# Hybrid decoder block on one core: the last projection as seven half-size products, with its weight prepared earlier

## The chip, the cores and the metric

One of the eight cores of a Trainium2 chip runs the kernel. The time is that of the device for one execution, in microseconds (us); the compared number is the median of several runs. TensorE multiplies matrices into PSUM, VectorE, ScalarE and GpSimd work on tiles, and sixteen DMA engines move data; SP and ScalarE issue the DMAs from queues that are worked off in order.

## The reference: what is computed

A residual block over 2048 positions of width 1024, all float32: one input projection of the normed input to 8192 columns, a recurrent branch, a dilated attention branch, two branch projections, a merge, and the last projection with a gated residual and a norm.

```python
mod = c_act @ w_mod[l] + b_mod[l]
shift, scale, gate = jnp.split(mod, 3, axis=-1)
h = rms_norm(x, g_norm[l]) * (1.0 + scale[:, None, :]) + shift[:, None, :]
proj = h @ w_in[l]
...
y_rnn = (hr * jax.nn.silu(z_rnn.astype(jnp.float32))).astype(dt) @ w_out_rnn[l]
...
y_attn = (o * jax.nn.silu(z_attn.astype(jnp.float32))).astype(dt) @ w_out_attn[l]
merged = jax.nn.sigmoid(g_r + bg_r) * y_rnn + jax.nn.sigmoid(g_a + bg_a) * y_attn
x = x + gate[:, None, :] * (merged @ w_o[l])
return rms_norm(x, g_final)
```

## The kernel before

Every float32 product is made of three fast matmuls: an operand is split into a high part (a copy to the rounded type, on ScalarE, `hi_act`, L157) and a low part (the difference, on GpSimd `lo_pool`, L163, or VectorE `lo_dve`, L166), and `mm3` (its matmuls all have line 149) adds high x high, high x low and low x high in PSUM. "A split" below means this pair of operations. A matmul has 128 rows of contraction and up to 512 columns.

**Input projection, two halves** (`f` = 0 and 1, each 1024 positions). A half has three stages. First the value products (`value_runs`), while VectorE and ScalarE build the half's operands (`build_odd`, L568 to L590); `second_values` (L862) holds the second half's plan: 8 runs of 4 slots, 24 matmuls of 256 columns a slot, and `plan[t, i]` lists what is issued behind each slot. Then the other columns in pairs of 128, by seven products of half-size blocks in place of eight (`strassen`): names B11, T2, T3, T1, B21, T4, B22, accumulators X, Z, W, V, Y in PSUM, 4 x 3 matmuls of 512 columns a product. 22 pairs lie in the recurrent stage, 6 in the rotary stage (pool `qp`). Operands are loaded and split some products ahead (`events`, `LEAD` = 4; in the second half `load_next` keeps seven tiles ahead, from `sD` or, unsplit, from the input weight). `later(d, fn)` and `after_prod` issue a step d products later. `output_weights` (L435) splits the two branch weights and stores them to `wD`, one part (load, split, store) every 6 products from the second half's start. `residual_gate` (L1253) computes the gate row of `mod` in the second half's rotary stage: eight 1024-wide loads `gw`, eight adds `gacc` on VectorE, two sums over partitions on TensorE, then the row is stored to `gateD`.

**Attention, with the branch projections as filler.** The generator `steps` (L1727) makes 8 jobs: `w_out_rnn` for four blocks of 512 positions, then `w_out_attn` for four. A job has 8 tiles (128 output channels x 512 positions), a tile 8 steps of one `mm3` into a `pj` bank (two banks). Steps are fed in between attention's work (`spend`). A tile's code at step k: at k = 1 and 5 a weight half is loaded (`load_w`), at k = 1 the tile before is evicted by VectorE with the gate tiles `fg` (L1789, L1791), at k = 3 the gates are loaded (`load_g`; four `fg` buffers, two a tile), at k = 7 the tile before is stored to `meT` (L1796). Operand rows `y` are loaded and split ahead (`load_y`, `split_y`). Jobs 0 to 5 lie under attention; a weight half is then read ready split from `wD`.

**The last stretch.** Jobs 6 and 7 read raw weight halves (`wr`, L1743) and split them. `output_operands` (L1901) loads `w_o` by rows, multiplies it with the gate row (L1905) and splits it (`oh`, `ol`). `output(n)` (L1909) takes one group of 128 positions after the other: load x and merged rows `mraw`, split them (`mh`, `ml`), 2 x 8 `mm3` into `pq`, add to x (L1927), square and sum (L1930), the inverse root, scale by it and by `g_final` (L1932), store. Job 7's steps are put between the first groups. This stretch lies outside the hand-written order (`manual_schedule`), so the compiler places its instructions.

Of the kernel before, what the change touches and what calls it, by code (L numbers as in the profile page):

```python
# [20 lines left out]
P = 128  # L21
# [68 lines left out]
def decoder_block(ctx, tc, x, c, positions, g_norm, w_mod, b_mod, w_in, b_gate, conv_w, conv_b,  # L90
# [24 lines left out]
    gateD = scratch("gateD", [1, D])  # L115

# [318 lines left out]
    def output_weights():  # L435

        parts = [(i, w, m, half) for i, w in enumerate((w_out_rnn, w_out_attn)) for m in range(KT) for half in range(2)]
        for x, (i, w, m, half) in enumerate(parts):
# [17 lines left out]
            for d, fn in ((1, load), (4, split), (6, store)):  # L456
                after_prod.setdefault(n_prod[0] + 6 * x + d, []).append(fn)
# [404 lines left out]
    def second_values():  # L862
# [22 lines left out]
        plan[7, 0].append(lambda: next(odd, None))  # L885
        value_runs(vx, ((0, 2), (1, 2), (2, 2), (3, 2), (3, 3), (0, 3), (1, 3), (2, 3)), plan, [])
# [366 lines left out]
    def residual_gate(ep):  # L1253
        acc = T(ep, [P, D], F32, "gacc")
        row = T(ep, [1, D], F32, "grow")
        nc.sync.dma_start(row[:], b_mod[0:1, 2 * D : 3 * D])
        w = {}

        def load(k):
            w[k] = T(ep, [P, D], F32, "gw", bufs=2)  # L1260
            nc.sync.dma_start(w[k][:], w_mod[0, k * P : (k + 1) * P, 2 * D : 3 * D])

        def add(k):
            t = w.pop(k)
            if k == 0:
                nc.vector.tensor_scalar(acc[:], t[:], ca[:, k : k + 1], None, ALU.mult)
            else:
                nc.vector.scalar_tensor_tensor(acc[:], t[:], ca[:, k : k + 1], acc[:], ALU.mult, ALU.add)

        def total(q):  # L1270
            w["pt"] = T(pg, [P, CH], F32, "pg")
            mm(w["pt"][:1, :], ones[:, 0:1], acc[:, q * CH : (q + 1) * CH], True, True)

        def bias(q):
            cq = slice(q * CH, (q + 1) * CH)
            nc.vector.tensor_tensor(row[:, cq], w["pt"][:1, :], row[:, cq], ALU.add)
            if q:
                nc.sync.dma_start(gateD, row[:])

        for k in range(KT):  # L1280
            later(1 + 3 * k, lambda k=k: load(k))
            later(6 + 3 * k, lambda k=k: add(k))
        for q in range(2):
            later(30 + 2 * q, lambda q=q: total(q))
            later(31 + 2 * q, lambda q=q: bias(q))
# [53 lines left out]
    for f in range(2):  # L1339
# [34 lines left out]
        if f:  # L1374
            residual_gate(qp)
# [348 lines left out]
    stored, whole = set(), []  # L1724


    def steps(jobs):  # L1727

        tiles = [(j, m) for j in range(len(jobs)) for m in range(KT)]
        Y, G = {}, {}  # L1730

        def load_w(x):

            if x < 2 * len(tiles):
                assert x == n_w[0]
                j, m = tiles[x // 2]
                if not whole:
                    load_wd(jobs[j][0], m, x % 2)
                    return

                n_w[0] += 1
                W[x] = T(pS, [P, 2, KH, P], F32R, f"S{x % 4}")
                t = T(whole[0], [P, KH, P], F32, "wr", bufs=3)  # L1743
                rows = slice(x % 2 * KH * P, (x % 2 + 1) * KH * P)
                nc.sync.dma_start(t[:], (w_out_rnn, w_out_attn)[jobs[j][0]][0, rows, m * P : (m + 1) * P]
                                  .rearrange("(k p) m -> p k m", p=P))
                hi_act(W[x][:, 0], t[:])
                (lo_dve if x % 2 else lo_pool)(W[x][:, 1], t[:], W[x][:, 0])

        def new_y(j, k):  # L1750
            Y[j, k] = [T(fl, [P, CH], F32R, tag, bufs=NY) for tag in ("yh", "yl")]
            return Y[j, k]

        def load_y(j, k):
            if j < len(jobs):
# [6 lines left out]
                if k in (1, 2, 3, 4):  # L1762
# [39 lines left out]
        for t, (j, m) in enumerate(tiles):  # L1802
            ps = T(pj, [P, CH], F32, "pj")
            for k in range(KT):
                if k % KH == 1:

                    load_w(2 * t + k // KH + 3)
# [4 lines left out]
                if k == 7 and t:  # L1812
# [161 lines left out]
```

## Time and profile before

| | us |
|---|---|
| three runs | 2258.34, 2264.17, 2263.09 |
| their median | 2263.09 |
| the profiled execution | 2262.75 |
| its span in the profile | 2260.8 |
| TensorE busy in the span | 2215.7 |
| mean granted TensorE clock | 0.993 |

The profile gives, for one execution, when each instruction ran, what ended an engine's idle time before it, and when each DMA was issued and landed. A row of a group of instructions has the line, the engine, the operation, output <- input (tile names without numbers), the shape and the count; then the busy time, the mean duration in ns of one, and the idle time of the engine before them with what ended it. Matmuls overlap, so the time of one (390 ns or so) is longer than the distance to the next. PEld is TensorE's weight load, which lies beside its matmuls.

### The profile page before, as it was taken

Reading aid. Unit: us, or ns where it says so; the run is one execution under the profiler, and the core shown is the slowest. Engines: PE = TensorE matmul, PEld = TensorE weight load, DVE = VectorE, ACT = ScalarE, POOL = GpSimd, SP = SyncE. Lnnn points to the kernel's source line nnn. Section 1 sums busy time; section 2 is a strip of 40 time slices with the busy share of each in tenths; the row PEclk is TensorE's granted clock in tenths of the full one; section 3 lists DMA queues with packets and bytes.
Section 4 is the critical chain, followed back from the end, with each engine's and each line's share of the span. In section 5 each row is a group of like instructions: output and inputs, shape, how many; then the busy total and the mean of one; then the engine's idle time right before and its main releaser. Section 6 shows DMA issues by size and latency. Waiting matters only on the chain.

```text
span 2260.8 us, 34143 instructions
## 1 busy us (share of the span) xinstructions
PE 2215.7 (98%) x11454; PEld 1862.4 (82%) x11455; DVE 1397.7 (62%) x2384; ACT 1271.4 (56%) x2475; POOL 1098.1 (49%) x816
## 2 busy tenths in 40 slices
PE   8999999999999999999999999999999999989998
PEld 5998888888877988888888887888888898877886
DVE  5578788777567555455545354466677877666443
ACT  3547667678543546657657412567678877533211
POOL 2267677676567454444444232446566666432100
PEclk9999999999999999999999999999999999999999
DMA  8354665565797456777776999989988797898542
GB/s 283 89 170 170 198 216 179 189 223 191 246 285 222 134 174 214 238 232 224 233 237 215 291 314 280 288 272 281 276 270 259 236 280 228 252 333 264 153 132 88
DMA packets 457235, 512.04 MB, mean 226 GB/s; under 512 B 89606, under 2 KB 341218, under 8 KB 456036
## 3 DMA queue, kind: packets, MB, share of 16 engines
q1 hardware_dynamic: 430452, 431.02, 63.0%
q10 hardware_dynamic: 26416, 78.81, 9.1%
q8 instruction: 90, 1.47, 0.3%
q14 instruction: 85, 0.70, 0.1%
q0 software_dynamic: 192, 0.05, 0.0%
HBM read 336.73 MB, written 173.02 MB: 225 GB/s over the span
## 4 chain that ended last, share of the span: by engine, by line
PE 51%; DMA 8%; DVE 4%; issue 2%; POOL 2%; SPq 1%; ACT 1%; POOLq 0%; ACTq 0%; DVEq 0%
PE pj L149 9%; PE X L149 8%; PE pq L149 7%; PE V L149 7%; PE Z L149 4%; PE W L149 4%; PE Y L149 3%; PE o L149 3%; PE sc L149 3%; DMA vraw<-vN 1%; PE pg L149 1%; PE pT L1574 1%; DMA wr<-in_w_out_attn_dram 1%; DMA S<-wD 1%; DMA yl<-oT 1%
## 5 line engine op out<-in xcount | busy, mean ns | idle before, releaser
L163 POOL TENSOR_TENSOR S<-R,S 128x512 fp32r<-128x512 f32 x246 | 365.2, 1490 | 358.8 <-ACT S L157 308.9
L149 PE MATMUL pj<-yh,S 128*128 128x512 f32 x1024 | 343.1, 395 | 6.9 <-ACT yh L157 4.8
L149 PE MATMUL X<-T,S 128*128 128x512 f32 x1344 | 332.2, 396 | 2.8 <-ACT S L157 1.5
L149 PE MATMUL V<-T,S 128*128 128x512 f32 x1344 | 331.3, 395 | 0.0
L149 PEld LDWEIGHTS X<-T,S 128*128 128x128 f32 x1344 | 253.2, 189 | 64.1 <-ACT S L157 2.5
L149 PEld LDWEIGHTS V<-T,S 128*128 128x128 f32 x1344 | 252.2, 188 | 58.6
L149 PEld LDWEIGHTS pj<-yh,S 128*128 128x128 f32 x1024 | 193.3, 189 | 48.1 <-ACT yh L157 6.0
L157 ACT ACTIVATE S<-R 128x512 fp32r<-128x512 f32 x246 | 150.9, 622 | 107.1 <-DMA R<-in_w_in_dram 92.9
L149 PE MATMUL pj<-yl,S 128*128 128x512 f32 x512 | 201.5, 394 | 2.6 <-DVE yl L166 1.6
L163 POOL TENSOR_TENSOR S<-s,S 128x512 fp32r<-128x512 f32 x84 | 128.5, 1530 | 112.3 <-ACT S L157 82.5
L1490 ACT ACTIVATE pp<-pp,st 128x256 f32<-128x256 f32 (+3 forms) x256 | 133.3, 522 | 74.8 <-DVE st L1489 74.4
L149 PE MATMUL Y<-T,S 128*128 128x512 f32 x672 | 165.5, 395 | 0.0
L149 PE MATMUL W<-T,S 128*128 128x512 f32 x672 | 165.5, 395 | 0.0
L149 PE MATMUL Z<-T,S 128*128 128x512 f32 x672 | 165.5, 395 | 0.0
L149 PEld LDWEIGHTS W<-T,S 128*128 128x128 f32 x672 | 126.3, 188 | 30.3 <-DMA R<-in_w_out_attn_dram 0.9
L149 PEld LDWEIGHTS Z<-T,S 128*128 128x128 f32 x672 | 126.5, 188 | 29.9
L149 PEld LDWEIGHTS Y<-T,S 128*128 128x128 f32 x672 | 126.5, 188 | 29.5
L958 DVE SCALAR_TENSOR_TENSOR xc<-xr,par,xc 128x512 f32<-128x512 f32 x96 | 98.6, 1028 | 50.4 <-ACT xc L952 48.1
L166 DVE TENSOR_TENSOR ptl<-pT,pth 128x384 fp32r<-128x384 f32 (+1 forms) x160 | 97.7, 627 | 48.6 <-ACT pth L157 46.3
L1489 DVE CUSTOM_DVE_ANT_0 pp<-sc,msk 128x256 f32<-128x256 f32 (+3 forms) x256 | 104.1, 448 | 35.5 <-PE sc L149 33.3
L1554 ACT ACTIVATE pp<-pp,M 128x256 f32<-128x256 f32 (+3 forms) x256 | 118.1, 524 | 9.2 <-DVE M L1678 9.2
L163 POOL TENSOR_TENSOR kq<-kraw,kq 128x512 fp32r<-128x512 f32 (+1 forms) x64 | 101.3, 1593 | 40.7 <-ACT kq L157 31.2
(332 smaller groups left out, 4725.2 us busy)
## 6 DMA issues: line engine op xcount, KB each, us to landing
sD<-S ACTq DMA_DIRECT2D x118, 512.0 KB, 3.7
S<-sD SPq DMA_DIRECT2D x118, 512.0 KB, 4.8
S<-wD SPq DMA_DIRECT2D x99, 512.0 KB, 5.8
R<-in_w_in_dram SPq DMA_DIRECT2D x196, 256.0 KB, 4.1
wD<-s ACTq DMA_DIRECT2D x64, 256.0 KB, 5.1
T<-in_w_mod_dram SPq DMA_DIRECT2D x8, 1024.0 KB, 12.1
vN<-ev SPq DMA_DIRECT2D x64, 128.0 KB, 2.0
zaT<-ev SPq DMA_DIRECT2D x32, 256.0 KB, 2.8
```

The costliest lines, as they stand in the source:

```text
L149: nc.tensor.matmul(o, lhsT=l, rhs=r, start=st, stop=sp, **kw)
L157: nc.scalar.activation(o, i, AF.Copy)
L163: nc.gpsimd.tensor_tensor(o, i, h.bitcast(F32), ALU.subtract)
L166: nc.vector.tensor_tensor(o, i, h.bitcast(F32), ALU.subtract)
L958: nc.vector.scalar_tensor_tensor(xc, xr[:, i : i + CH], cw(i), xc, ALU.mult, ALU.add)
L1489: nc.vector.tensor_tensor_reduce(pdst, s_ps, mask, 1.0, 3e38, ALU.add, ALU.min, m_)
L1490: nc.scalar.activation(pdst, pdst, AF.Exp, bias=m_, scale=-1.0, accum_out=l_)
L1554: nc.scalar.activation(pp, pp, AF.Copy, scale=w)
L1574: nc.tensor.transpose(pt[:, c0 + j * P : c0 + (j + 1) * P], pp[i][:, k * P : (k + 1) * P], ident)
```

## The change

- **The last projection by seven products.** `output_products` takes two groups of 128 positions and both 512-column halves of the weight at a time, by the scheme of `strassen`: 8 pairs x 7 products x 12 matmuls. The merged rows are loaded, summed (VectorE) and split (ScalarE, GpSimd) some products ahead (`jobs`, `LEAD`); GpSimd adds the shared sums u2 and u3 to x; V alternates between a bank of its own and one of `pj`. The last pair has shorter final operations (`finish_last`).
- **The gate row** is computed during the second half's value products, in 512-column halves: a load `gw` behind one slot, the add three slots later.
- **The gated weight.** `gated_weight`, in the second half's rotary stage, loads `w_o` in four groups of rows, multiplies it with the gate row, forms the sums that the seven products need and stores seven parts to `oD` on ScalarE's queue. They are loaded and split late, during jobs 6 and 7 (`load_o`, `hi_o`, `lo_o`), the last eight of 28 splits behind the first products.
- **Jobs 6 and 7 share each weight**: their tiles alternate (two and two at the start), and a weight half is loaded and split once for both; 12 halves are raw, the others come from `wD`. Their store comes at k = 5.
- **The branch weights'** parts come every 19/4 products, not every 6.
- All of the last stretch now lies in the hand-written order. `output_operands`, `output` and the pools `pq` and `wr` are gone.

```diff
-                after_prod.setdefault(n_prod[0] + 6 * x + d, []).append(fn)
+                after_prod.setdefault(n_prod[0] + 19 * x // 4 + d, []).append(fn)
...
+        residual_gate(vx, plan)
         value_runs(vx, ((0, 2), (1, 2), (2, 2), (3, 2), (3, 3), (0, 3), (1, 3), (2, 3)), plan, [])
...
+    def residual_gate(ep, plan):
...
-        for k in range(KT):
-            later(1 + 3 * k, lambda k=k: load(k))
-            later(6 + 3 * k, lambda k=k: add(k))
+            nc.vector.tensor_tensor(row, w["pt"][:1, :], row, ALU.add)
+            nc.scalar.dma_start(gateD[:, q * CH : (q + 1) * CH], row)
+
         for q in range(2):
-            later(30 + 2 * q, lambda q=q: total(q))
-            later(31 + 2 * q, lambda q=q: bias(q))
+            for k in range(KT):
+                i = 2 + 13 * q + (3 * k) // 2
+                at_slot(i, lambda q=q, k=k: load(q, k))
+                at_slot(i + 3, lambda q=q, k=k: add(q, k))
+            at_slot(5 + 13 * q, lambda q=q: nc.sync.dma_start(row, b_mod[0:1, 2 * D + q * CH : 2 * D + (q + 1) * CH]))
+            at_slot(16 + 13 * q, lambda q=q: total(q))
+            at_slot(17 + 13 * q, lambda q=q: bias(q))
...
+    def gated_weight(ep):
...
+            def gate(i):
+                tt(v[i][:].rearrange("p j c -> p (j c)"), v[i][:].rearrange("p j c -> p (j c)"), gate_b[:], ALU.mult)
...
+            def store_rows():
+                nc.scalar.dma_start(oD[k, :, 0, :], v[0][:, 0, :])
+                nc.scalar.dma_start(oD[k, :, 1:3, :], v[1][:])
+
+            def store_sums():
+                nc.scalar.dma_start(oD[k, :, 3:6, :], v["t"][:])
+                nc.scalar.dma_start(oD[k, :, 6, :], v["t3"][:].rearrange("p k m -> p (k m)"))
+
+            return ((0, load), (3, lambda: gate(0)), (4, lambda: gate(1)), (5, store_rows), (5, lambda: sums(0)),
+                    (6, lambda: sums(1)), (8, store_sums))
+
+        for k, i in enumerate((1, 10, 19, 28)):
+            for d, fn in group(k):
+                later(i + d, fn)
...
-            residual_gate(qp)
+            gated_weight(qp)
...
+        tiles = [(j, m) for j in range(LAST_HEAD) for m in range(KT)]
+        tiles += [(LAST_HEAD + i, m) for i in range(2) for m in range(2)]
+        tiles += [(LAST_HEAD + i, m) for m in range(2, KT) for i in range(2)]
...
+        raw_at, split_at = {}, {}
+        for x in range(RAW_W, 2 * KT * (LAST_HEAD + 1)):
+            m, h = divmod(x - 2 * KT * LAST_HEAD, 2)
+            u = 2 * KT * LAST_HEAD + h + (2 * m + 1 if m < KH else 4 * m - 5)
+            split_at[u], raw_at[u - 3] = x, x
...
+                if k == (7 if j < LAST_HEAD else 5) and t:
...
+                    i = (t - KT * LAST_HEAD) * KT + k
+                    if i < 2:
+                        split_y(j, 5 + i)
+                    if i in (0, 1, 2, 3, 6, 7):
+                        load_y(j + 1, i + 2 if i < 4 else i)
+                    if i in (1, 2, 5, 6, 8, 9, 11, 12):
+                        split_y(LAST_HEAD + 1, (1, 2, 5, 6, 8, 9, 11, 12).index(i))
...
+    def output_products(fill):
...
+        B_ORDER = "B11", "T2", "T3", "T1", "B21", "T4", "B22"
+        for i in range(24):
+            a = 10 + 9 * i // 2
+            at_step(a, lambda i=i: load_o(i))
+            if i < 20:
+                at_step(a + 8, lambda i=i: hi_o(i))
+                at_step(a + 10, lambda i=i: lo_o(i))
+        at_step(118, lambda: load_o(24))
...
+            return ((-6, lambda: raw("a11", 0, 0)), (-5, lambda: raw("a21", 1, 0)), (-4, lambda: raw("a22", 1, 1)),
+                    (-1, lambda: raw("a12", 0, 1)), (0, sums), (0, lambda: split(0, "a11")),
+                    (1, lambda: tt(v["a21"], v["a11"], v["a21"], ALU.subtract)), (1, lambda: split(1, "s2")),
+                    (2, lambda: split(2, "a21")), (3, lambda: split(3, "s1")), (4, lambda: split(4, "a12")), (2 if x else 4, load_x),
+                    (5, lambda: tt(v["s2"], v["a12"], v["s2"], ALU.subtract)),
+                    (5, lambda: split(5, "a22")), (6, lambda: split(6, "s2")))
...
+        def product(ps, name, start, stop, i):
+            (bh, bl), t = F[name], first.pop(i)
+            for k in range(KH):
+                mm3(ps[:], t[:, 0, k, :], t[:, 1, k, :], bh[:, k, :], bl[:, k, :],
+                    first=start and k == 0, last=stop and k == KH - 1, skip_group_check=True)
+            done_n[0] += 1
+            run_jobs(done_n[0])
...
+        for x in range(len(order)):
+            X = T(pf, [P, CH], F32, "X", bufs=2)
+            product(X, "B11", True, False, 7 * x)
+            while held:
+                held.pop()()
+            Z = T(pf, [P, CH], F32, "Z")
+            product(Z, "T2", True, True, 7 * x + 1)
+            u1 = T(gp, [P, CH], F32, "u1", bufs=1)
+            u2 = T(gp, [P, CH], F32, "u2", bufs=2)
+            nc.scalar.activation(u1[:], X[:], AF.Copy)
+            tt(u2[:], Z[:], u1[:], ALU.add)
+            add_x(x, 0, 1, u2)
+            Wp = T(pf, [P, CH], F32, "W")
+            product(Wp, "T3", True, True, 7 * x + 2)
+            u3 = T(gp, [P, CH], F32, "u3", bufs=1)
+            tt(u3[:], Wp[:], u2[:], ALU.add)
+            add_x(x, 1, 1, u3)
+            add_x(x, 1, 0, u3)
+            V = T(pj, [P, CH], F32, "pj") if x % 2 else T(pf, [P, CH], F32, "V")
+            product(V, "T1", True, False, 7 * x + 3)
+            finish(x, 1, 1, V, u3)
+            product(X, "B21", False, True, 7 * x + 4)
+            finish(x, 0, 0, X, None)
+            Y = T(pf, [P, CH], F32, "Y")
+            product(Y, "T4", True, True, 7 * x + 5)
+            finish(x, 1, 0, Y, u3)
+
+            def last(x=x, V=V):
+                product(V, "B22", False, True, 7 * x + 6)
+                finish(x, 0, 1, V, None)
+            held.append(last)
+        held.pop()()
+        run_jobs(10 ** 6)
+        pools.close("gp", "pf", "fp", "pR", "pS", "pjb")
...
+        pools.close("ap", "sc", "pT", "po")
+        output_products(fill)
```

In `operands`, the numbers are products relative to the pair's first, less `LEAD`; a negative result falls on the last of the 128 steps (100 to 124).

341 lines of the change are left out of this document (240 added, 101 removed).

## The prediction

> **What bounds the kernel now.** I read the page first, then the chain of work that ended last, then the busy time by windows, then the waits and the rows in order of time at three places that the change touches. The page's first part comes first.
>
> ```profile
> PE 2215.7 (98%) x11454; PEld 1862.4 (82%) x11455; DVE 1397.7 (62%) x2384; ACT 1271.4 (56%) x2475; POOL 1098.1 (49%) x816
> ```
>
> TensorE is the bound: 45.1 of 2260.8 us are idle, so a change gains by taking matmuls away or by filling one of the few gaps, and loses by opening a new one. The last stretch, from the end of attention, reads as follows: the chain's rows at both ends, the matmuls of the last two jobs (`pj`) by window, and the group of one third of the output matmuls (`pq`; two more groups have the same x256).
>
> ```profile
> 1971.03 5.54 PE pj L149 x24
> ...
> 2165.23 87.06 PE pq L149 x384
> ```
> ```profile
> 1971.00:2000.00 29.00, 25.69 (x105) 20.46 (x105) 2.75 (x4) 0.94 0.97 320
> 2000.00:2020.00 20.00, 10.32 (x45) 8.06 (x44) 1.35 (x2) 0.91 1.09 327
> 2020.00:2040.00 20.00, 16.57 (x71) 12.98 (x70) 1.37 (x2) 1.00 1.00 313
> 2040.00:2060.00 20.00, 8.32 (x34) 5.85 (x32) 1.35 (x2) 1.00 0.97 303
> 2060.00:2165.20 105.20, 39.27 (x168) 31.57 (x168) 4.82 (x7) 1.00 0.55 169
> 2165.20:2261.00 95.80, 0.03 (x1) 0.00 (x0) 0.69 (x1) 0.97 0.34 113
> ```
> ```profile
> L149 PE MATMUL pq<-oh,mh 128*128 128x512 f32 x256 | 100.4, 393 | 3.0 <-ACT mh L157 3.0
> ```
>
> The undisturbed pace is 87.06 / 384 = 0.2267 us a matmul. From 1971.03 to 2252.29 are 281.3 us for 424 `pj` and 768 `pq` matmuls; at that pace they take 1192 x 0.2267 = 270.2. So **11 us are lost** there, before 2060, where the DMA share is 0.97 to 1.09 at 303 to 327 GB/s. The rest, 8.5 us up to 2260.8, is the tail.
>
> **The change part by part.** The sum is made against the profiled run's 2262.75 us (span 2260.8 and 1.95 around it), 0.3 us under the median of the three runs, 2263.09.
>
> *1. Seven products.* Before: 16 row groups x 2 halves x 8 x 3 = 768 matmuls. After: 8 pairs of row groups x 7 products x 4 x 3 = 672. The input projection runs such products already:
>
> ```profile
> 899.66 2.96 PE L149 MATMUL X<-T,S 128*128 128x512 f32 x12
> 902.45 2.95 PE L149 MATMUL Y<-T,S 128*128 128x512 f32 x12
> ```
>
> One follows the other by 2.79 us, 0.2325 a matmul, with splits four products ahead as in the new code; I take that pace. 672 x 0.2325 = 156.2 against 768 x 0.2267 = 174.1: **-17.9 us** (-21.8 at the old pace). What hides the rest: for a pair, 19.5 us of TensorE, GpSimd has 7 splits and 3 adds. At the first row's 1.49 and the second's 1.70 us a pass, below, that is 14.9 to 17.0 us.
>
> ```profile
> L163 POOL TENSOR_TENSOR S<-R,S 128x512 fp32r<-128x512 f32 x246 | 365.2, 1490 | 358.8 <-ACT S L157 308.9 <-issue 13.4 <-DMA R<-in_w_in_dram 10.4
> L163 POOL TENSOR_TENSOR S<-wr,S 128x512 fp32r<-128x512 f32 x14 | 23.8, 1700 | 82.7 <-ACT S L157 82.7
> ```
>
> VectorE has 4 operand sums, 6 evictions, 4 scalings and small ones, some 12 us. The first pair adds 4 late splits of the weight to GpSimd; the operands are due four products (11 us) later, so I cost that at nothing. V alternates between two banks: its eviction cannot hold the next T1.
>
> *2. The last two jobs.* 128 steps of 3 matmuls, as before. Gone are 17 of the 29 loads and splits of a raw weight, the four-megabyte load of `w_o` with its gating, and the interleaved output. New are 26 loads of gated parts (256 KB) and their splits. In these 87 us the code now moves 16 tiles x 768 KB of gates, sums and stores, 12 raw weights, 26 parts, some 14 operand loads: about 26 MB, 300 GB/s, just under the 303 to 327 above. So it stays near the limit. What ends last here is a loop on SP: the gate load of a tile waits for the store two tiles back (four `fg` buffers), and the store of the tile before stands behind that load.
>
> ```profile
> fg<-gaT SPq DMA_DIRECT2D x11, 256.0 KB, 5.7
> ...
> meT<-fg SPq DMA_DIRECT2D x10, 256.0 KB, 5.5
> ```
> ```profile
> SPq L1784 <- DMA meT<-fg: 9.0, 4, 3.7
> ```
>
> A tile lasts 24 x 0.2267 = 5.44 us; the loop takes 0.9 (two issues) and a store's 4 to 5.5, so 4.9 to 6.4. I take 5.8 over 14 tiles, 5 us, and 3 us at the start, as in the row of 1985.08 below, for `y` loads that now wait for a raw buffer to be split: **8 us lost instead of 11, -3** (bounds: 3 lost, or 17 if the loop is 6.5 throughout).
>
> *3. The tail.*
>
> ```profile
> 2253.08 1.06 ACT L1930 ACTIVATE ob<-xo 128x1024 f32<-128x1024 f32 x1 [9.30 <-DVE xo L1927]
> ...
> 2255.65 1.28 DVE L1932 SCALAR_TENSOR_TENSOR ob<-xo,ss,gf 128x1024 f32<-128x1024 f32 x1
> ```
>
> The last square and the last scaling now have 512 columns: half of 1.06 and 1.28 saves 1.2, one more small add costs 0.2: **-1 us** (bounds 0 and -2).
>
> *4. The gate row, now in the second half's value products.* Here VectorE builds the odd operands in one almost unbroken run, and what follows hangs on its end.
>
> ```profile
> 780.00:800.00 20.00, 20.00 (x170) 20.00 (x170) 19.13 (x19) 9.56 (x17) 13.87 (x9) 1.00 0.44 129
> 800.00:820.00 20.00, 20.00 (x170) 20.00 (x169) 17.73 (x16) 8.23 (x15) 12.34 (x8) 1.00 0.17 50
> ```
> ```profile
> 817.25 0.63 ACT L157 ACTIVATE T<-t 128x512 fp32r<-128x512 f32 x1 [3.97 <-DVE t L589]
> 817.78 0.58 ACT L766 ACTIVATE ev<-W 128x512 f32<-128x512 f32 x1
> ```
> ```profile
> 820.41 3.64 DMA R<-in_w_in_dram
> ...
> 824.14 0.64 ACT S L157
> ...
> 824.85 1.28 POOL S L163
> ...
> 826.17 2.59 PE X L149 x10
> ```
>
> Behind a window stand its length, the busy time of PE, PEld, DVE, ACT and POOL, the clock, the DMA share and GB/s: VectorE is busy for 19.1 and 17.7 of 20 us. ScalarE's split waits for it, the eviction stands behind the split, the value store behind the eviction, the next operand's load behind the store on SP. The added operations:
>
> ```profile
> L1268 DVE SCALAR_TENSOR_TENSOR gacc<-gw,ca,gacc x7: 1259/1277/1299, 1302.3 to 1354.5; 128x1024 f32<-128x1024 f32 x7
> L149 PE MATMUL pg<-gacc,ones x4: 590/590/591, 1362.9 to 1370.1; 128*1 128x512 f32 x4
> ```
>
> The 512-wide form is half, 0.66. The first eight adds (slots 5 to 15) lie in light VectorE time and cost nothing. Of the second eight, six and one bias come ahead of the last operand: 0.67 + 0.4 + 5 x 0.66 = 4.4 us, so that end moves from 817.2 to 821.6. Then `total(1)` waits on TensorE, in slot 29 (about 818.5), for the last two adds: 824.4. Behind it are slots 30 and 31, of 24 matmuls and 2.85 us each by the first two rows here, 5.7 us. A wait of that length has a second price, in the other rows:
>
> ```profile
> 820.35 1.59 PE L149 MATMUL V<-S,T 128*128 128x256 f32 x12
> 821.78 1.58 PE L149 MATMUL X<-S,T 128*128 128x256 f32 x12
> ```
> ```profile
> 1985.08 0.49 PE L149 MATMUL pj<-yh,S 128*128 128x512 f32 x1 [3.08 <-ACT yh L157]
> ...
> 1987.25 0.63 PE L149 MATMUL pj<-yl,S 128*128 128x512 f32 x1
> 1987.67 1.05 PE L149 MATMUL pj<-yh,S 128*128 128x512 f32 x2
> ```
>
> After 3.08 us of idling the matmuls start 0.43 us apart, about ten of them, 2 us lost. So: 824.4 + 1 (the sum's two matmuls) + 5.7 + 2 = 833, against 826.2: **+7 us** (0 if VectorE's gaps take the adds; +12 with each of the seven at 1.67, below). The Trainium skill, "TensorE: Matmul & The Clock Gate", Part 1, says that an idle window of about 3.4 us halves the clock and about 3.4 us of work restores it; by that rule the same 1.7 us are due here, and the row above agrees.
>
> ```profile
> 778.65 0.69 DVE L576 TENSOR_TENSOR hx<-hx,T 128x512 f32<-128x512 f32 x1
> 779.38 1.67 DVE L578 TENSOR_TENSOR hx<-hx,T 128x512 f32<-128x512 f32 x1
> ```
>
> The same shape takes 0.69 or 1.67. The Trainium skill, "SBUF — State Buffer", section "SBUF: two separate sides", has a cause: VectorE with two SBUF inputs and GpSimd exclude each other for a whole instruction. By it an added sum may itself be held; the number of GpSimd passes stays the same, so I stay at 0.66.
>
> *5. The rotary stage without the gate row.* Its four matmuls leave a full TensorE: **-1.9 us** (0.9 at the common pace, 2.4 at 0.59 each).
>
> *6. The gated weight in the rotary stage.* Added: 4.5 MB of loads, 7.3 MB of stores on ACT's queue, 8 gatings and 16 sums on VectorE. Removed: 4 MB of gate-row loads, and six parts of the output weights (768 KB each, 4.9 MB with the ends), which the tighter spacing (19/4 products, not 6) moves ahead of it. Net +2.9 MB where the share of the DMA is already full:
>
> ```profile
> 1240.00:1260.00 20.00, 20.00 (x88) 16.22 (x87) 10.63 (x14) 13.51 (x20) 7.04 (x6) 1.00 0.86 274
> ...
> 1300.00:1320.00 20.00, 20.00 (x87) 16.22 (x87) 10.22 (x15) 3.86 (x7) 5.32 (x4) 1.00 1.07 335
> 1320.00:1340.00 20.00, 20.00 (x87) 16.21 (x87) 11.65 (x16) 4.21 (x8) 8.53 (x6) 1.00 0.96 316
> 1340.00:1360.00 20.00, 20.00 (x87) 16.18 (x86) 10.17 (x14) 1.86 (x3) 4.81 (x3) 1.00 0.98 294
> ```
>
> TensorE does not idle there: operands are loaded seven products (19.5 us) ahead. That cover takes the 2.9 MB (9 us at 315 GB/s) once. VectorE has 10 of 20 us free; a group's gating waits at worst a few us for its load, and the tightest deadline behind it, V's eviction, is two products (5.6 us). I take **+1.5 us** (0 to +9). The earlier spacing in the recurrent stage costs nothing: its TensorE is full, and its DMA share, 0.86 at its end in the first row, has room.
>
> *Sum:* -17.9 - 3 - 1 + 7 - 1.9 + 1.5 = -15.3; 2262.75 - 15.3 = **2247 us**.
>
> **The rivals.**
> - *All covered* (2236): the loop holds at 5.4, the adds find gaps: 3 lost in step 2 (-5), 1 instead of 7 in step 4. For it: VectorE's run is paced by its own waits here and there. Against: 19.1 of 20.
> - *SP's loop binds the last two jobs* (2259): 6.5 a tile and the start give 17 + 3 lost, 12 more than forecast. For it: the 5.5 and 5.7 us landings at full DMA. Against: landings shrink when TensorE slows.
> - *GpSimd becomes the bound of the products* (2251): at 2 us a pass, ten passes are 20 us against 19.5, 0.5 a pair, 4 in all.
> - *The full DMA delays the rotary stage* (2255): all 2.9 MB show, 9 us instead of 1.5.
> - *Slower than before* (2272): the gate row's loads pace the adds. There are two `gw` buffers, so a load is issued only after the add two before it, on SP behind value stores that wait for ScalarE, which waits for VectorE. It decides when queue and landing (4 us by the 3.64 above) exceed the three slots (8.5 us) given; then each of six adds holds VectorE by about 4 us: +25. Against it: the DMA share is 0.17 to 0.44 there.
>
> **How the numbers follow.** Forecast 0.52, all covered 0.14, SP's loop 0.16, GpSimd 0.08, rotary DMA 0.04, paced adds 0.06. About 0.3% (6.8 us) is what a measurement of this kernel can tell from no change, so faster means under 2256.3. The forecast, all covered, GpSimd, and parts of SP's loop and rotary DMA lie there: 0.80. Most of SP's loop: 0.13 the same. Paced adds and the worst ends: 0.07 slower. The range reaches from just below all covered to SP's loop, 2234 to 2260; the ends of all bounds together, 2228 and 2271, are left out.
>
> **What would show it.** Step 1: 672 output matmuls in groups of 12 that start 2.79 us apart. Step 2: TensorE idle between 1971 and the first product, with SP waiting for `meT`. Step 4: a TensorE wait of 5 us or so on VectorE before the second half's first product, and a clock under 1 behind it. Step 6: no TensorE waits before the first fill step. The forecast is wrong if the product stage waits for GpSimd, if step 4 shows no wait, or if the fill loses over 15 us.

## The result, and the profile after

The changed kernel takes **2277.7 us** (median of 6 runs, 2273.8 to 2282.3), the kernel before 2264.9 us beside it: a ratio of 1.0059, with a 95% interval of 1.0038 to 1.0080. It is slower by 0.6%; faster, by 0.7%, was forecast. The profiled execution took 2277.55 us with a span of 2275.6, so its rows can be held against those of before, 2262.75 and 2260.8. Most lines of the changed kernel have moved: the matmul helper is L150, the splits are L158 (high part, ScalarE), L164 and L167 (low part, GpSimd and VectorE).

The first part of its page:

```profile
PE 2203.7 (97%) x11358; PEld 1844.9 (81%) x11359; DVE 1462.2 (64%) x2471; ACT 1294.1 (57%) x2560; POOL 1204.4 (53%) x902
```

TensorE has 96 matmuls less and is busy for 12.0 us less, as the change meant, but it now idles for 71.9 us of the span instead of 45.1. To find where, I took the starts of the same events in both traces, in order of time. First two rows of before (first fill step after the projection, last matmul of attention), then the rows of after: the second half's first product, the first fill step, attention's end, the first and the last of the seven products.

```profile
1398.58 0.39 PE L149 MATMUL pj<-yh,S 128*128 128x512 f32 x1
...
1970.76 0.27 PE L149 MATMUL o<-pth,vh 128*128 128x128 f32 x1
```
```profile
834.70 2.94 PE L150 MATMUL X<-T,S 128*128 128x512 f32 x12
...
1409.97 0.39 PE L150 MATMUL pj<-yh,S 128*128 128x512 f32 x1
...
1981.82 0.27 PE L150 MATMUL o<-pth,vh 128*128 128x128 f32 x1
...
2086.43 2.94 PE L150 MATMUL X<-F,S 128*128 128x512 f32 x12
...
2262.72 3.01 PE L150 MATMUL pj<-F,S 128*128 128x512 f32 x12 [1.09 <-DVE xo L2081]
```

| stretch | before | after | change | forecast |
|---|---|---|---|---|
| to the second half's first product (before: 826.17, the row of ten of its twelve matmuls) | 826.2 | 834.7 | +8.5 | +7 (step 4) |
| from it to the first fill step | 572.4 | 575.3 | +2.9 | -0.4 (steps 5, 6) |
| attention | 572.2 | 571.9 | -0.3 | 0 |
| last two jobs, 424 matmuls (before: 281.3 less 174.1, as the output lay among them) | 107 | 104.6 | -3 | -3 (step 2) |
| the last projection | 174.1 | 179.3 | +5.2 | -17.9 (step 1) |
| tail | 8.5 | 9.9 | +1.4 | -1 (step 3) |

The table gives +15 us where the two executions differ by 14.8. **The seven products are the miss**: 672 matmuls were to take 156.2 us and take 179.3, 23 us more. A window of after in that stage (columns as before: length, then PE, PEld, DVE, ACT and POOL, clock, DMA share and GB/s), and the longest of TensorE's waits there (us in total, times, longest):

```profile
2160.00:2180.00 20.00, 17.82 (x76) 13.94 (x75) 14.85 (x27) 6.82 (x16) 12.10 (x10) 1.00 0.40 130
```
```profile
PE X L150 <- ACT u L2154: 9.5, 7, 1.5
PE V L150 <- DVE xo L2113: 3.9, 4, 1.6
PE pj L150 <- DVE xo L2113: 2.2, 3, 0.7
```

No engine is full: TensorE works for 17.8 of 20 us, VectorE for 14.8, GpSimd for 12, ScalarE for 7. A pair of row groups takes some 22 us instead of 19.5, with seven waits of B21 for the copy `u1` of X's first product and seven of B22 for the eviction of T1's result out of V's bank into `xo`. The chain behind one of them, in order of time:

```profile
2158.75 3.00 POOL L164 TENSOR_TENSOR S<-R,S 128x512 fp32r<-128x512 f32 x2
2158.85 0.15 DVE L171 TENSOR_SCALAR ss<-ss 128x1 f32<-128x1 f32 x1
...
2160.71 1.06 DVE L177 TENSOR_TENSOR ss<-ss 128x1 f32<-128x1 f32 x1
2161.71 1.29 POOL L164 TENSOR_TENSOR S<-s,S 128x512 fp32r<-128x512 f32 x1
2161.80 1.22 DVE L178 TENSOR_TENSOR ss<-ss 128x1 f32<-128x1 f32 x1
...
2164.77 0.68 DVE L2113 TENSOR_TENSOR xo<-V,xo 128x512 f32<-128x512 f32 x1
2165.55 0.63 ACT L2124 ACTIVATE jk<-xo 128x512 bf16<-128x512 f32 x1 [4.22 <-DVE xo L2113]
...
2166.68 0.20 ACT L172 ACTIVATE ss<-ss 128x1 f32<-128x1 f32 x1 [0.41 <-DVE ss L171]
2166.79 0.58 ACT L2154 ACTIVATE u<-X 128x512 f32<-128x512 f32 x1
...
2167.42 3.04 PE L150 MATMUL X<-F,S 128*128 128x512 f32 x12 [1.44 <-ACT u L2154]
```

Read it from the end. The product B21 goes into the bank X, which `u1` must have read (2167.42). That copy stands on ScalarE behind the square of the pair before (2165.55) and the root that follows it (2166.68); the square waited for VectorE's eviction of V (2164.77). And VectorE came late to it because, ahead of it, operations on a single column, 128x1, took 1.06 and 1.22 us. Their ends give the reason: 2160.71 + 1.06 = 2161.77 and 2161.80 + 1.22 = 2163.02, each 0.02 us behind the end of a GpSimd pass (2158.75 + 3.00 for two, and 2161.71 + 1.29). The one with a single tensor input, L171, took 0.15 in the middle of a pass. In the kernel before, the same operation (there L176) took 0.16 us, in a stage where GpSimd was busy for 10.4 of 200 us:

```profile
L176 DVE TENSOR_TENSOR ss<-ss 128x1 f32<-128x1 f32 x14 | 2.2, 159 | 0.5
```
```profile
2060.00:2260.00 200.00, 192.27 (x848) 158.87 (x846) 82.81 (x169) 38.06 (x67) 10.37 (x5) 0.99 0.45 143
```

The groups of after (from 2107 to 2260) sum it up; busy time, mean ns of one:

```profile
L177 DVE TENSOR_TENSOR ss<-ss 128x1 f32<-128x1 f32 x14 | 15.1, 1077 | 0.5
L178 DVE TENSOR_TENSOR ss<-ss 128x1 f32<-128x1 f32 x14 | 9.6, 687 | 0.5
```

With L2126 and L180 these are 56 operations on a column with two tensor inputs. In the trace, 29 of them began while a GpSimd pass ran: all 29 took 1.03 to 1.28 us and ended 0.01 to 0.02 us behind the end of a pass. The other 27 began between passes and took 0.16. The sums of operands, 512 wide, stretch too: L2033 and L2022 take 1.67 and 1.61 us on average, where the same shape takes 0.69 alone.

**Theory A**: the products are slowed by a loop in order over VectorE, ScalarE and GpSimd, lengthened by the small operations that wait out a GpSimd pass. **Rival B**, the rival of the prediction: GpSimd, with seven splits and three adds a pair, is the bound.

The other two places. The second sum of the gate row waits on TensorE as forecast, and the clock falls behind it; in the rotary stage and at the first fill step (`yh`) there are waits that the forecast did not have:

```profile
825.47 1.87 PE L150 MATMUL pg<-s,ones 128*1 128x512 f32 x2 [8.39 <-DVE s L1274]
```
```profile
820.00:840.00 20.00, 14.53 (x73) 11.85 (x74) 5.36 (x7) 5.18 (x9) 4.65 (x4) 0.74 0.68 203
```
```profile
PE pj L150 <- ACT yh L158: 3.3, 1, 3.3
PE V L150 <- DVE t L466: 1.9, 1, 1.9
PE X L150 <- ACT S L158: 1.5, 1, 1.5
```

### The profile page after: what moved, and what is told of

Same layout as the page of the kernel before. It is cut to its first block, busy times and chain, and to the rows that moved or that the text cites. A ratio compares the mean times of both kernels' runs of the same rounds, so it can differ in the third digit from the quotient of the medians.

```text
span 2275.6 us, 34370 instructions
## 1 busy us (share of the span) xinstructions
PE 2203.7 (97%) x11358; PEld 1844.9 (81%) x11359; DVE 1462.2 (64%) x2471; ACT 1294.1 (57%) x2560; POOL 1204.4 (53%) x902
## 5 line engine op out<-in xcount | busy, mean ns | idle before, releaser
L164 POOL TENSOR_TENSOR S<-R,S 128x512 fp32r<-128x512 f32 x278 | 408.8, 1476 | 407.4 <-ACT S L158 383.0
L150 PE MATMUL X<-T,S 128*128 128x512 f32 x1344 | 331.1, 395 | 3.3 <-ACT S L158 1.5
L150 PE MATMUL V<-T,S 128*128 128x512 f32 x1344 | 331.4, 395 | 2.0 <-DVE t L466 2.0
L150 PE MATMUL pj<-yh,S 128*128 128x512 f32 x896 | 303.5, 397 | 6.1 <-ACT yh L158 3.3
L150 PEld LDWEIGHTS X<-T,S 128*128 128x128 f32 x1344 | 252.6, 188 | 63.6 <-ACT S L158 1.9
L150 PEld LDWEIGHTS V<-T,S 128*128 128x128 f32 x1344 | 252.1, 188 | 61.1 <-DVE t L466 2.3
L158 ACT ACTIVATE S<-R 128x512 fp32r<-128x512 f32 x278 | 170.8, 622 | 157.0 <-DMA R<-in_w_in_dram 95.0
L164 POOL TENSOR_TENSOR S<-s,S 128x512 fp32r<-128x512 f32 x108 | 159.6, 1477 | 121.5 <-ACT S L158 92.3
L150 PEld LDWEIGHTS pj<-yh,S 128*128 128x128 f32 x896 | 170.3, 190 | 41.2 <-ACT yh L158 3.7
L150 PE MATMUL pj<-yl,S 128*128 128x512 f32 x448 | 177.2, 396 | 1.6 <-DVE yl L167 1.2
L150 PE MATMUL Y<-T,S 128*128 128x512 f32 x672 | 165.5, 395 | 0.0
L150 PE MATMUL Z<-T,S 128*128 128x512 f32 x672 | 165.5, 395 | 0.0
L150 PE MATMUL W<-T,S 128*128 128x512 f32 x672 | 165.4, 395 | 0.0
L150 PEld LDWEIGHTS Z<-T,S 128*128 128x128 f32 x672 | 126.6, 188 | 29.8
L150 PEld LDWEIGHTS Y<-T,S 128*128 128x128 f32 x672 | 126.5, 188 | 29.4
L150 PEld LDWEIGHTS W<-T,S 128*128 128x128 f32 x672 | 126.4, 188 | 29.4
L158 ACT ACTIVATE S<-s 128x512 fp32r<-128x512 f32 x108 | 67.4, 624 | 125.7 <-DVE s L290 31.1
L167 DVE TENSOR_TENSOR ptl<-pT,pth 128x384 fp32r<-128x384 f32 (+1 forms) x160 | 97.7, 627 | 48.9 <-ACT pth L158 46.6
```

The costliest lines, as they stand in the source:

```text
L150: nc.tensor.matmul(o, lhsT=l, rhs=r, start=st, stop=sp, **kw)
L158: nc.scalar.activation(o, i, AF.Copy)
L164: nc.gpsimd.tensor_tensor(o, i, h.bitcast(F32), ALU.subtract)
L167: nc.vector.tensor_tensor(o, i, h.bitcast(F32), ALU.subtract)
```

## The experiments

Times are medians; a ratio is to the kernel before on the same chip. Where stages of two profiled executions are compared, a few us can be chance: attention, the same code in all, took 570.1 to 574.6 us in eleven of the twelve.

### The copy u1 earlier (e1_u1_early)

```
             product(X, "B11", True, False, 7 * x)
+            u1 = T(gp, [P, CH], F32, "u1", bufs=1)
+            nc.scalar.activation(u1[:], X[:], AF.Copy)
             while held:
...
-            u1 = T(gp, [P, CH], F32, "u1", bufs=1)
...
-            nc.scalar.activation(u1[:], X[:], AF.Copy)
```

> One part alone: ScalarE's copy u1 of the first product of a pair is issued right after that product, ahead of the held product B22 and of T2, so that it no longer stands behind the square of the pair before. Theory A (the output products are slowed by a loop in order over VectorE, ScalarE and GpSimd, none of them full; the square waits for an eviction, u1 waits for the square, B21 waits for u1): the seven waits of X for u1, 9.5 us, go, a part comes back as waits of V and pj for xo; about -8 us, 2270 us, between 2266 and 2274. Rival B (GpSimd, with seven splits and three adds a pair, is the bound of the products): the pair still lasts about 22 us, 2276 to 2279.

2274.7 us, ratio 1.0059 (1.0040 to 1.0078), the same ratio as the changed kernel's. TensorE's longest waits in the products:

```profile
PE V L150 <- DVE xo L2113: 6.5, 4, 1.6
PE pj L150 <- DVE xo L2113: 4.3, 3, 1.6
```

The seven waits for `u1` are gone, and half of their 9.5 us is back at the evictions (6.5 + 4.3 instead of 3.9 + 2.2). In the profiled run the products take 173.5 us instead of 179.3, but the time, just above theory A's 2266 to 2274, shows no gain that can be told. The gain was over-estimated: the order on ScalarE is a part of the loop, and what makes VectorE late remains. Rival B is not ruled out by this run.

### The small operations with one tensor input (e2_small_ops)

```
+    def rstd_last1(ss):
...
+        nc.vector.tensor_scalar(t, y, y, None, ALU.mult)
+        nc.vector.tensor_scalar(t, t, v, None, ALU.mult)
...
+        nc.vector.tensor_scalar(y, y, t, None, ALU.mult)
...
-                    tt(ss[:, 0], ss[:, 0], ss[:, 3], ALU.add)
+                    nc.vector.tensor_scalar(ss[:, 0], ss[:, 0], ss[:, 3], None, ALU.add)
...
-                rstd_last(ss)
+                rstd_last1(ss)
```

> One part alone: the four 128x1 operations with two tensor inputs for each row group (the sum of the squares and three of the root's step) become operations of one tensor with a per-partition scalar, the same arithmetic. Theory A with the second input as the cause of their stretch (1.08, 0.69 and 0.67 us instead of 0.15): each takes about 0.15 to 0.2 us, VectorE loses some 29 us of busy time in the output products, and the waits of X, V and pj shrink: -6 to -14 us, about 2268. If the stretch has another cause, the rows stay at 0.7 to 1.1 us and the time at 2276 to 2279. Rival B (GpSimd is the bound): the rows shrink and the time stays at 2276 to 2279.

**2264.9 us**, ratio 0.9998 (0.9980 to 1.0016): 13 us below the changed kernel. Two of the four rewritten groups (L2134 is the sum of the squares, L185 the square of the root), all that TensorE still waits for in the products with the row of the longer wait, and a window:

```profile
L2134 DVE TENSOR_SCALAR ss<-ss 128x1 f32<-128x1 f32 x14 | 3.0, 214 | 18.9 <-ACT jk L2132 18.9
...
L185 DVE TENSOR_SCALAR ss<-ss 128x1 f32<-128x1 f32 x14 | 3.0, 214 | 0.5
```
```profile
PE X L150 <- POOL S L164: 3.0, 1, 3.0
PE V L150 <- POOL F L164: 0.2, 1, 0.2
```
```profile
2113.61 4.63 PE L150 MATMUL X<-F,S 128*128 128x512 f32 x10 [2.98 <-POOL S L164]
```
```profile
2160.00:2180.00 20.00, 20.00 (x89) 16.32 (x88) 14.84 (x30) 7.91 (x20) 15.79 (x11) 1.00 0.53 169
```

1.08 us (L177 of the changed kernel) has become 0.21 with GpSimd busier than before, 15.8 of 20 us, every wait for `u1` and `xo` is gone, and TensorE works for 20 of 20 us. Of the same 56 operations (2107 to 2250) 50 now begin during a GpSimd pass, and none takes more than 0.22 us. The products take 161.6 us (2093.4 to 2254.9). This decides for theory A and against B: GpSimd does the same passes, in a shorter stage. VectorE lost 19 us of busy time there (130.7 to 111.5), not the 29 expected: the scalings with two tensor inputs that follow (L2133, now L2141) rose from 0.75 to 1.01 us on average. TensorE still waits at one place, the second pair's start, for low parts on GpSimd. The Trainium skill, "SBUF — State Buffer", section "SBUF: two separate sides", has the rule: a VectorE operation with two SBUF inputs and a GpSimd operation that reads SBUF exclude each other for a whole instruction. The trace agrees (1.08 us beside 0.16), and shows what follows from it for a column: the wait is that of a 512-wide pass, however small the operation.

### Two of seven low parts on VectorE (e3_two_lows)

```
-                lo_pool(t[:, 1], v[name], t[:, 0])
+                (lo_dve if i in (2, 5) else lo_pool)(t[:, 1], v[name], t[:, 0])
```

> Two of the seven low parts of a pair go from GpSimd to VectorE, so GpSimd loses some 3 us of a pair and VectorE gains as much. Rival B (GpSimd is the bound of the products): faster, by 8 pairs of up to 2.5 us, to 2258 to 2270. Theory A (VectorE's order in front of the evictions is what is late): VectorE's queue grows by 2 x 1.7 us a pair and the waits for xo and u grow: slower by 4 to 16 us, 2282 to 2294; no change would speak against both.

2278.2 us, ratio 1.0069 (1.0050 to 1.0088): no change, which by the expectation speaks against both theories as they stood. In the profiled run the products take 175.1 us instead of 179.3; TensorE's wait for `u1` fell to half, those for `xo` stayed:

```profile
PE X L150 <- ACT u L2154: 4.8, 6, 0.8
```
```profile
L167 DVE TENSOR_TENSOR S<-R,S 128x512 fp32r<-128x512 f32 x14 | 12.8, 913 | 1.0 <-ACT S L158 1.0
...
L178 DVE TENSOR_TENSOR ss<-ss 128x1 f32<-128x1 f32 x13 | 3.1, 240 | 0.4
```

VectorE got 12.8 us of low parts and lost as much elsewhere (131.3 us busy in the products, 130.7 in the changed kernel): L178 alone went from 9.6 to 3.1 us, and the operand sums L2033 from 11.7 to 5.8, with 18 us less of GpSimd passes beside them. So theory A needed a correction: as far as operations with two inputs go, work moved from one of the two engines to the other still takes turns with what is left there. The Trainium skill, "Perfetto Trace Analysis", section "Optimizing Scalar/DVE Operations", says that moving operations between these two may not help for that reason; this run agrees.

### The gate row's adds earlier in the value products (e4_gate_early)

```
-                i = 2 + 13 * q + (3 * k) // 2
+                i = 9 * q + k
...
-                at_slot(i + 3, lambda q=q, k=k: add(q, k))
+                at_slot(i + 2, lambda q=q, k=k: add(q, k))
...
-            at_slot(16 + 13 * q, lambda q=q: total(q))
+            at_slot(10 + 14 * q, lambda q=q: total(q))
```

> One part alone: the sixteen adds of the gate row are issued one a slot in slots 2 to 18 of the second half's value products instead of 5 to 28, ahead of most of VectorE's odd operands, and the second sum waits until slot 24. Theory (the 8.4 us that the second sum waits for VectorE, behind its full run, is the loss of this step): that wait goes, the first product of the second half starts at 826 to 828 instead of 834.7, about -8 us, 2269 to 2271. Rival (the adds cost VectorE their time wherever they stand, because the run of odd operands is full to its end): the first product starts at 831 or later, 2274 to 2278.

2281.2 us, ratio 1.0085 (1.0070 to 1.0100): nothing won. The last odd operand's split on VectorE, and the first product of the second half:

```profile
826.20 0.69 DVE L167 TENSOR_TENSOR T<-t,T 128x512 fp32r<-128x512 f32 x1 [0.70 <-ACT T L158]
```
```profile
833.09 4.83 PE L150 MATMUL X<-T,S 128*128 128x512 f32 x12 [5.09 <-ACT S L158]
```

The sum's wait is gone, but VectorE's run of odd operands now ends at 826.9 (818.6 in the kernel before), the split and the load behind it are late instead, and the first product ends at 837.9, where it ended at 837.6 in the changed kernel. The rival was right in what it said of the row, though the time lies 3 us above its 2274 to 2278: in both placements that were run, the adds cost their time.

### The gate row in the recurrent stage (e5_gate_later)

On top of the short small operations, sixteen chunks of 64 columns:

```
-        residual_gate(vx, plan)
...
+                nc.vector.tensor_tensor(t, t, ca[:, :KT].unsqueeze(2).broadcast_to([P, KT, QW]), ALU.mult)
+                nc.vector.tensor_reduce(v["a"][:], t.rearrange("p k c -> p c k"), AX.X, ALU.add)
...
+                mm(v["pt"][:1, :QW], ones[:, 0:1], v["a"][:], True, True)
```

> On top of e2_small_ops (2264.9 us): the gate row leaves the value products and is summed in the second half's recurrent stage, in sixteen chunks of 64 columns, one load, one product with a broadcast and one reduction on VectorE, one small matmul; the bias is added to the broadcast row in the rotary stage. Theory (what the step costs is the adds' time in VectorE's run of odd operands, wherever in that run they stand): without them the first product of the second half starts at 825 to 828 us instead of 836.4, VectorE's free half in the recurrent stage hides the sums, sixteen small matmuls cost some 2 to 3 us: 2256 to 2260. Rival (the second half starts late for another reason, say the loads of the next stage): the first product stays at 834 or later, 2265 to 2269.

2262.5 us, ratio 1.0001 (0.9991 to 1.0012), in neither range. The kernel with short small operations and one bank for V, below, ran beside it on the same chip and took 2262.7, so nothing was won. The first product starts at 823.5 after a wait, as the theory said and a little earlier, 11 us earlier than in the changed kernel, and yet the first fill step, at 1412.2, is not earlier:

```profile
823.49 4.14 PE L150 MATMUL X<-T,S 128*128 128x512 f32 x10 [0.61 <-POOL S L164]
...
1412.15 0.40 PE L150 MATMUL pj<-yh,S 128*128 128x512 f32 x1
```
```profile
937.95 2.95 PE L150 MATMUL V<-T,S 128*128 128x512 f32 x12
940.83 0.27 PE L150 MATMUL pg<-gacc,ones 128*1 128x64 f32 x2
...
943.92 2.95 PE L150 MATMUL Y<-T,S 128*128 128x512 f32 x12
```

Products follow each other by 2.79 us; here V to Y is 5.97 instead of 5.58. One sum of 64 columns costs a full TensorE 0.4 us, sixteen cost 6, more than the 2 to 3 that I had put down. In the rotary stage V waits 4.5 us once more. So the start of the second half is late because of the adds in VectorE's run, and this way out was paid for in another place.

### The gating on GpSimd; and three quarters of the traffic left out (e6_gating_pool, e7_no_o_traffic)

```
-                tt(v[i][:].rearrange("p j c -> p (j c)"), v[i][:].rearrange("p j c -> p (j c)"), gate_b[:], ALU.mult)
+                for j in range(2):
+                    nc.gpsimd.tensor_tensor(v[i][:, j, :], v[i][:, j, :], gate_b[:, j * CH : (j + 1) * CH], ALU.mult)
```

> On top of e2_small_ops (2264.9 us): the eight gatings of the output weight in the rotary stage go from VectorE to GpSimd, which is mostly free there. Theory C (part of the rotary stage's waits is V's eviction standing behind two gatings in VectorE's order, 1.4 us; the rest, 2.5 and 0.7 us, is late operand loads): V's wait for t goes, X's waits for S stay, -1 to -2 us, 2263 to 2264. Rival D (all of the waits, 4.6 us, come from VectorE's order): all three go, 2260. Rival E (a gating on GpSimd holds VectorE's two-input operations and the low parts as long): new waits, 2266 to 2270.

2263.9 us, ratio 1.0004 (0.9991 to 1.0017): no change that can be told. V's wait for `t` did not go, it is 3.4 us. The time fits theory C, the wait does not, so this run ruled for none of the three.

```
             def load():
                 for i in range(2):
+                    if k:
+                        v[i] = kept[i]
+                        continue
...
             def store_rows():
+                if k:
+                    return
...
-            nc.sync.dma_start(raw_o[i][:], oD[k, :, O_PART[B_ORDER[name]], :])
+            nc.sync.dma_start(raw_o[i][:], oD[0, :, O_PART[B_ORDER[name]], :])
```

> On top of e2_small_ops (2264.9 us), with part of the work left out: three of the four groups of the output weight are neither loaded nor stored in the rotary stage (their gatings and sums run on the first group's tiles, and the output products load the first group's parts four times). Theory C (X's waits for S, 2.5 and 0.7 us, are operand loads made late by the gated weight's loads and stores, 9 MB of the stage's traffic): these two go, V's wait for t stays, -3 us, 2262. Rival D (VectorE's order): all waits stay, 2264 to 2266.

**2252.4 us**, ratio 0.9958 (0.9943 to 0.9973), 10 us below the run of the next section beside it, which has the same stage with all its traffic. What TensorE waits for from 1296 to 1500, in that run and then without the traffic:

```profile
PE X L150 <- ACT S L158: 2.5, 1, 2.5
PE pj L150 <- ACT yh L158: 2.0, 1, 2.0
...
PE V L150 <- DVE t L474: 1.3, 1, 1.3
```
```profile
PE sc L150 <- DVE xq L1726: 1.4, 1, 1.4
PE pj L150 <- DVE yl L167: 1.2, 1, 1.2
```

All waits of the rotary stage are gone, V's for VectorE too, though VectorE did the same gatings and sums; so is that at the first fill steps. It was the DMA, and more of it than theory C had said: with the traffic, VectorE's gatings wait 18.3 us in all for their loads of `w_o` (four waits), and V's eviction stands behind them in order. From the first product to the first fill step the profiled run takes 570.5 us, where the run with the traffic takes 577.5; attention takes 566.7 instead of 570.3, of which 2.0 is the wait at the first fill steps and the rest no more than attention scatters by.

### One bank for V (e8_one_bank)

```
-            V = T(pj, [P, CH], F32, "pj") if x % 2 else T(pf, [P, CH], F32, "V")
+            V = T(pf, [P, CH], F32, "V")
```

> On top of e2_small_ops (2264.9 us), one part undone: every pair's V lies in the same bank. From B22 of a pair to T1 of the next are two products, 5.6 us, and the eviction takes 0.69 us in a VectorE that is 13 of 20 us busy. Theory (the second bank is a margin that nothing uses once the small operations are short): no wait of V for xo, 2264 to 2266. Rival (it is needed): V waits for xo in most pairs, 1 to 2 us each, 2272 to 2280.

2262.7 us, ratio 1.0000 (0.9988 to 1.0013), one wait of V for `xo`, 0.3 us. With the small operations short, the second bank is a margin that next to nothing uses.

### Two sums instead of sixteen, and all together (e9_two_sums, e10_with_u1)

The chunks' sums are stored as they are and added up in the rotary stage; the second kernel adds the early `u1`.

```
+                nc.scalar.dma_start(accD[:, q * QW : (q + 1) * QW], v["a"][:])
...
+        nc.gpsimd.memset(both[:], 1.0)
...
+            mm(pt[:], both[:], acc[:, q, :], True, True)
...
-        for k, i in enumerate((1, 10, 19, 28)):
+        for k, i in enumerate((6, 14, 22, 29)):
```

> e5_gate_later again, but the sixteen small matmuls and evictions go: the chunks' partial sums are stored to DRAM as they come, loaded whole at the start of the rotary stage, and two matmuls with a 128x128 matrix of ones sum and broadcast them; the groups of the gated weight start five products later. Theory F (e5_gate_later won its 12 us at the start of the second half and lost them again by the end of the rotary stage, about 6 us by sixteen matmuls of 0.27 us that each hold TensorE by some 0.4 us, and the rest by V's wait of 4.5 us behind the late gate row): 2253 to 2257, and from the first product of the second half to the first fill step 575 to 579 us instead of 584.5. Rival G (the loss is the chunks' loads in pieces of 256 bytes or VectorE's 32 us of sums): 582 or more, 2260 to 2264.

> e9_two_sums with the early copy u1 of e1_u1_early. With the small operations short, the output products of e2_small_ops showed no wait of X for u1, V or pj for xo. Theory A (one chain in order; once it is shorter than the pair, its order no longer matters): as e9_two_sums, within 2 us. Rival (the two losses add up): 3 us or more below it.

**2258.5 us**, ratio 0.9970 (0.9955 to 0.9985), and **2254.0 us**, ratio 0.9953 (0.9935 to 0.9970). In the first, from the start of the second half to the first fill step:

```profile
824.22 4.13 PE L150 MATMUL X<-T,S 128*128 128x512 f32 x10 [0.63 <-POOL S L164]
...
1402.36 0.40 PE L150 MATMUL pj<-yh,S 128*128 128x512 f32 x1
```

578.1 us instead of 588.7 in the run with sixteen sums, counted from the start of the same row (574.0 instead of 584.5 from its end, as the expectation counts). Rival G, 582 or more, is out. Theory F has the size and the place, though this lies 1 us below its range and the time 1.5 us above; the sixteen matmuls and the late gate row were changed together, so their shares are not told apart. The second kernel lies 4.5 us below the first, on the rival's side, but their intervals overlap and its profiled run is the longer one (span 2251.9 beside 2247.9). The products themselves take 160.7 us in the first and 160.1 in the second, as theory A would have it, so where the 4.5 us come from, if they are more than chance, stays open. Both beat the kernel before, by 0.3% and 0.5%.

## Why the prediction was wrong

It forecast 2247 us (2234 to 2260) and gave slower a chance of 0.07.

- **Step 1 failed, in its sentence on what hides the rest**: GpSimd 14.9 to 17.0 us of a pair's 19.5, VectorE some 12, so it "costs nothing". The count of matmuls and their pace were right: in the second experiment the products follow each other 2.77 us apart once the second pair has begun. GpSimd's sum was right as well (14.6 us a pair in the changed kernel, 15.6 in the second experiment). But the cover was counted by engine, as sums against the pair's time. What decided was a loop through the engines in order, where V's eviction stands behind two row groups' small operations, ScalarE's square behind the eviction, `u1` behind the square, and B21 behind `u1`. And VectorE's time was not 12 but 16.3 us a pair: the operations on one column with two inputs, taken as "small ones", cost some 37 us of the stage (15.1 and 9.6 for the two groups shown, 9.4 and 3.1 for two more), where 56 of them at 0.16 would cost 9. The rows of before gave nearly all of them at 0.16, with GpSimd idle. But two began beside one of its passes at the end of the last two jobs, and the one at 2065.83 took 1.10: it is the greatest of the three durations (least, median and greatest, in ns) in the row of L179 below. The change put GpSimd to work beside all of them. The exclusion was quoted in step 4 for another stage and not carried to this one. GpSimd as the bound of the whole stage, the rival with 0.08, is refuted by the second experiment.

```profile
L179 DVE TENSOR_TENSOR ss<-ss x17: 158/159/1103, 676.6 to 2255.5; 128x1 f32<-128x1 f32 x16, 128x4 f32<-128x4 f32 x1
```

- **A second part of step 1 failed**: the first pair's late work, costed "at nothing" as its operands are due four products later. In the changed kernel the two products at the second pair's start take 10.7 us (2103.01 to 2113.74) instead of 5.6, with waits of 1.7 for a split on GpSimd, 1.6 for an eviction and 1.1 for a late split of the weight; in the second experiment they take 12.0. The split stands on GpSimd behind an add that waited 4.2 us for its load of x. Which of the loads and the late splits is to blame was not tried. So about 18 of the 23 us are the loop, 5 are this.
- **Step 2 was right in its sum, by luck in its terms**: 8.5 us lost in the last two jobs, 8 forecast (104.6 less 424 x 0.2267). From 2013.38 to the first product 13 tiles take 5.62 us each, not 5.8, so SP's loop costs 2.3 us and not 5. The start costs 6.2 instead of 3: TensorE waits 2.8 us for a weight half from `wD` and 1.5 for an eviction. The `y` loads that the prediction named stand around that weight load on SP's queue; whether they hold it was not tried.

```profile
1997.91 0.47 PE L150 MATMUL pj<-yh,S 128*128 128x512 f32 x1 [2.82 <-DMA S<-wD]
```

- **Step 3 had the wrong sign**: +1.4 instead of -1. In the chain that ended last stand one small operation of 1.20 us and one product with the weight row of 1.09, which take 0.16 and 0.69 where nothing holds them. The first ends just behind GpSimd's last three products with the weight row (2263.55 to 2267.31). In the second experiment it took 0.21, but the product 1.51, and the tail was 9.3 us, so most of the miss stays open.

```profile
2266.14 1.20 DVE ss L178
...
2268.34 1.09 DVE u L2090
```

- **Step 4 was right in its mechanism and a little small**: the sum's wait of 8.4 us, the slow clock behind it (0.74 in that window), first product at 834.7 instead of 833. The fourth experiment adds what the step did not say: issuing the adds earlier in that stage did not hide them.
- **Steps 5 and 6 together**: +2.9 instead of -0.4. "TensorE does not idle there" did not hold, nor did the cover by operands loaded seven products ahead. The rival *the full DMA delays the rotary stage* (9 us, chance 0.04) had the mechanism: without three quarters of the traffic the waits are gone. Its size is not measured by the 10 us, which are the price of some 8.6 MB left out, where the rival had the net 2.9 MB. The stretch takes 572.4 us in the kernel before, 575.3 to 578.2 in five profiled runs with the changed code, and 570.5 without that traffic, 1.9 below before, as step 5 had it for the four gate matmuls. If step 5 is taken at its 1.9, step 6 cost 5 to 8 us instead of 1.5. Step 5 was not tried by itself.
- *Paced adds*, the rival on the slower side, did not occur: VectorE's adds waited for no load. The kernel is slower mainly for a reason that no rival named.

Step 1 alone is 23 of the 30 us between forecast and result; steps 3, 4, 5 and 6 are the rest, 7.

## What to carry to other kernels

When a change puts a second engine to work beside small operations, price those operations again, by rows in which both engines are busy, and by the longest duration of a row as well as its mean; where one input can be given as a per-partition scalar, give it so. To show that a stage with no full engine keeps up, follow one buffer round its loop in program order (who writes it, what stands ahead of that on each engine, who waits), instead of adding up each engine's time. And moving an operation within an unbroken run on one engine may not hide it: here it had to leave the run.

## What the runs showed that I had not expected

A VectorE operation on 128x1 with two tensor inputs took 0.16 us alone and 1.03 to 1.28 when it began beside GpSimd's 512-wide passes, ending 0.01 to 0.02 us behind a pass; with a per-partition scalar as second operand it took 0.21 beside the same passes. A matmul of 64 columns in float32 that was not split, 0.27 us in its row, held a full TensorE for 0.4 us.
